# Two heads side by side: 64-wide products of a recurrence and an attention regrouped

## The chip, the cores and the metric

One core of one Trainium2 chip runs the whole program in one launch. The metric is device time in microseconds (us), the median of three runs. The engines are TensorE (PE in the rows; PEld is its weight load), VectorE (DVE), ScalarE (ACT), GpSimd (POOL) and SyncE (SP), which issues the loads of the weights.

## The reference, cut to what matters

Three transformer blocks follow each other on one sequence of 256 tokens with 2048 features, all in float32. Blocks 2 and 3 are not touched. Block 1 normalises x, multiplies by `w_in`, and runs two branches of 16 heads with 64 features each, a gated linear recurrence and an attention:

```python
# recurrence, a 64 x 64 state per head, token by token
kk = (k * k_k).reshape(B, S, H, N)
kk = kk / jnp.maximum(jnp.sqrt(jnp.sum(kk * kk, axis=-1, keepdims=True)), 1e-12)
def step(state, inp):
    rt, wt, kt, vt, kkt, at = inp
    sa = jnp.einsum('bhvk,bhk->bhv', state, -kkt)
    state = (state * wt[:, :, None, :] + sa[..., None] * (kkt * at)[:, :, None, :]
             + vt[..., :, None] * kt[..., None, :])
    return state, jnp.einsum('bhvk,bhk->bhv', state, rt)
# y is then normalised per token and head (mean and variance over its 64 features)

# attention of a chunk of 64 tokens to itself and the chunks before it
s = jnp.einsum('bqhd,bkhd->bhqk', qc, kc) + bias          # invalid keys: -1e30
p = jax.nn.softmax(s, axis=-1)
o = jnp.einsum('bhqk,bkhd->bqhd', p, vc)
```

## The kernel before, in words

`run` is the weight stream. Each weight tile of 128 × 1024 is loaded by SP, split into a high part `whi` (ScalarE, L209) and a low part `wlo` (VectorE, L210), and multiplied with an activation that stands as high and low parts too: L249 (512 columns) and L250 (256 columns) alternate on TensorE for each block of 128 × 128 weights. The four accumulators `pm` have four of the eight PSUM banks.

Everything else is a background task, a Python generator. After each unit of the stream (four pairs L249/L250 in the common form) `step` lets every task issue its next stage; `yield n` leaves out steps. So the work of a task stands between the stream's products in the order in which it was issued, and each engine works in that order; `run` and `step` write it out, no scheduler moves it. Tiles come from pools and wait for the release of the buffer that they get: `PS` (four PSUM banks for all background tasks), `X` (five tiles; the scores `sc`, `E`, `BT` and `UV` are among them), `T` (12), `Q` (30 large tiles).

`attention` starts one head every three steps: scores `psc` (two products on 64 rows of the array, the row half by the head's parity, L337, L338), bias and maximum on VectorE, exponentials on ScalarE, scaling on POOL, three transposes `ptr`, a copy, and two products with v into `ppv` (L365, L366), each head into its 64 columns. Block 1 calls it twice with eight heads (`att`); blocks 2 and 3 call it with heads of 128.

`rwkv(hf)` runs the recurrence of eight heads, so twice. Four tiles i hold two heads each (par 0 on partitions 0 to 63, par 1 on 64 to 127). First come the decay and rate from `w2` (`pw`, `pa`, L741, L742) and the inverse norm `rn` of kk, which four products per tile spread over the features (`pkk`, L786); the operands `AR` and `BK`; a triangular inverse `Z`. Then four chunks c of 64 tokens. `gram(c)` makes the masked products P (`pgr`, L912), `BT` (four full transposes `pbt`, L918) and v token-major (`pvt`, L925, products with pieces of the identity). The chunk then does `pW` (from the state S, L943, and from P, L945), `pU` (with Z, L954), the next state's `pS` (L964) and the output `pY` (from P, L978, and from the state, L981). `group_norm` normalises pY and turns it feature-major (`pyt`, L1030).

Of the kernel before, what the change touches and what calls it, by code (L numbers as in the profile page):

```python
# [10 lines left out]
ALU = mybir.AluOpType  # L11
# [6 lines left out]
# columns of the packed per-feature vectors (each vector of n features takes n / 128 columns)  # L18
# [27 lines left out]
class FM:  # L46
    """A feature-major tensor [128 * n, 256] as tiles of four rows of blocks."""
# [8 lines left out]
class HL:  # L56
    """An activation (hi | lo), two blocks of 128 features to a tile."""
# [8 lines left out]
class Builder:  # L66
# [102 lines left out]
    def get(self, key, f):  # L169
        """Block f of the (hi | lo) activation st[key], once it is on its way."""  # L170
# [3 lines left out]
    def start(self, gen):  # L174
        """First stage of what happens to a product; the further ones follow, one a step."""
# [4 lines left out]
    def run(self, panels):  # L180
# [39 lines left out]
        for i, (p, g) in enumerate(groups):  # L220
# [12 lines left out]
            # where, among the units of this group, the next group is split  # L233
# [34 lines left out]
    def sum_halves(self, p):  # L268
        """The product of a weight tile: its two halves in PSUM, added."""
# [8 lines left out]
    def split_act(self, dst, src):  # L278
        """dst (hi | lo) of src, both parts exact."""
# [4 lines left out]
    def scaled_split(self, dst, src, g):  # L284
        """dst (hi | lo) of src * g, g one number per partition."""
# [10 lines left out]
    def sum_sq(self, accs):  # L296
        """Sums over partitions and tiles ([128, 256] each), token-major, in PSUM [128, 2]."""
# [15 lines left out]
    def bcast_psum(self, rt):  # L313
        """A token-major [128, 2], over all partitions: [128, 256]."""
# [12 lines left out]
    def attention(self, heads, q, k, v, bias, dim, out):  # L327
        """Softmax attention of query tiles (tokens 0-127 on keys 0-127, 128-255 on 0-255).
        q, k: feature-major [dim, 256]; v(h, t): token-major [128, dim]; bias(h, s, p) is a task that
        writes s [128, 384] = scores + bias; out(i, psum [128, 256])."""  # L330
        nc = self.nc
        pvs, done = {}, []

        def head(h):
            p = self.PS("psc")
            qa, ka = q(h), k(h)
            nc.tensor.matmul(p[:, 0:128], qa[:, 0:128], ka[:, 0:128], start=True, stop=True)  # L337
            nc.tensor.matmul(p[:, 128:384], qa[:, 128:256], ka, start=True, stop=True)  # L338
            s = self.X("sc", [128, 384])
            yield from bias(h, s, p)  # L340
            mx = self.SM([128, 2], "mx")
            nc.vector.tensor_reduce(out=mx[:, 0:1], in_=s[:, 0:128], axis=AX.X, op=ALU.max, negate=True)
            nc.vector.tensor_reduce(out=mx[:, 1:2], in_=s[:, 128:384], axis=AX.X, op=ALU.max, negate=True)
            yield 2
            sm = self.SM([128, 2], "sm")
            nc.scalar.activation(s[:, 0:128], s[:, 0:128], AF.Exp, bias=mx[:, 0:1], accum_out=sm[:, 0:1])
            nc.scalar.activation(s[:, 128:384], s[:, 128:384], AF.Exp, bias=mx[:, 1:2], accum_out=sm[:, 1:2])
            yield 2
            rs = self.SM([128, 2], "rs")
            nc.vector.reciprocal(rs, sm)  # L350
            nc.gpsimd.tensor_scalar(s[:, 0:128], s[:, 0:128], rs[:, 0:1], None, op0=ALU.mult)
            nc.gpsimd.tensor_scalar(s[:, 128:384], s[:, 128:384], rs[:, 1:2], None, op0=ALU.mult)
            yield 3
            p = self.PS("ptr")
            nc.tensor.transpose(p[:, 0:128], s[:, 0:128], self.ident)
            nc.tensor.transpose(p[:, 128:256], s[:, 128:256], self.ident)
            nc.tensor.transpose(p[:, 256:384], s[:, 256:384], self.ident)
            yield 2
            nc.scalar.copy(s, p[:, 0:384])
            yield 2  # L360
            if dim == 128 or h % 2 == 0:
                pvs[h * dim // 128] = self.PS("ppv")
            pv = pvs[h * dim // 128]
            o = pv[(h * dim) % 128:(h * dim) % 128 + dim, 0:256]
            nc.tensor.matmul(o, v(h, 0), s[:, 0:256], start=True, stop=False, skip_group_check=True)  # L365
            nc.tensor.matmul(o[:, 128:256], v(h, 1), s[:, 256:384], start=False, stop=True,  # L366
                             skip_group_check=True)
            if dim == 128 or h % 2:
                yield 2
                out(h * dim // 128, pv[:, 0:256])  # L370
            done.append(h)

        for h in heads:
            self.bg(head(h))
            yield 3
# [4 lines left out]
    def block1_constants(self):  # L380
# [19 lines left out]
        # 1 - x of mu_r, mu_k, mu_v and of k_a  # L400
# [5 lines left out]
    def input_norm(self, x, gname, hl, key):  # L406
        """hl (hi | lo) of x * g, four blocks at a time, then st[key]: sums of squares."""
# [17 lines left out]
    def load_x(self, name, between=False):  # L425
        """x, feature-major; the later tiles between the first tiles of the weights, or at once."""
# [10 lines left out]
    def block1(self):  # L437
# [36 lines left out]
        # attention, eight heads at a time: q, k feature-major, v token-major  # L474
# [44 lines left out]
        # LoRA: (h + (shift(h) - h) mu) w = h ((1 - mu) w) + shift(h) (mu w)  # L519
# [23 lines left out]
        def mixed(key, n, hf):  # L543
            """y + (shift(y) - y) mu of the product y"""
# [25 lines left out]
        # gated attention branch  # L570
# [70 lines left out]
        # merged branches  # L641
# [59 lines left out]
    def residual(self, hl, gname, key):  # L701
        """x += rms(o) post_norm_g; hl of x * g for what follows; st[key] of 1 / rms(x)."""
# [24 lines left out]
    def rwkv(self, hf):  # L727
        """The recurrence of eight heads, in chunks of 64 tokens."""
# [4 lines left out]
        # decay and in-context rate  # L733
# [16 lines left out]
        # 1 / max(|k k_k|, 1e-12) per head  # L750
# [16 lines left out]
        rn = self.SM([128, 2, 8], "rn")  # L767
        nc.gpsimd.tensor_tensor(rn.rearrange("p t h -> p (t h)"), mn, self.mhalf[:, 0:16], op=ALU.pow)
# [7 lines left out]
        def operands(i):  # L776
# [46 lines left out]
        # (I - L)^-1 per head and chunk: diagonal blocks of 32 by substitution, one block per partition  # L823
# [58 lines left out]
        # the block below the diagonal: X21^T = X11^T L21^T X22^T  # L882
# [19 lines left out]
        # the recurrence over chunks  # L902
        Pt, BT, UV = {}, {}, {}

        def gram(c):
            P_ = Pt[c] = self.Q("P", [128, 2, 4, 128])
            m = self.mask1[:, None, :].to_broadcast([128, 4, 128])
            for par in range(2):
                o = slice(par * 64, par * 64 + 64)
                p = self.PS("pgr")  # L910
                for i in range(4):
                    nc.tensor.matmul(p[:, i * 128:(i + 1) * 128], bk(i, c)[o, :], ar(i, c)[o, :], start=True, stop=True)  # L912
                yield
                nc.vector.tensor_tensor(P_[:, par], p.rearrange("p (i t) -> p i t", i=4), m, op=ALU.mult)
# [6 lines left out]
            U_ = UV[c] = self.X("UV", [128, 4, 2, 64])  # L921
            p = self.PS("pvt")
            for i in range(4):
# [797 lines left out]
```

## Time and profile before

| | us |
|---|---|
| median of three runs | 3351.51 (3348.92 to 3356.8) |
| profiled execution: span from first to last instruction | 3342.3 |
| TensorE busy in it | 3288.9 (98%) |
| VectorE, ScalarE, POOL busy | 2066.9 (62%), 1716.4 (51%), 556.2 (17%) |
| mean granted TensorE clock, as a share of 2.4 GHz | 0.994 |

The profile gives no other time of the profiled execution than its span. Its rows show a float32 product of the code as two records on TensorE (two passes over the columns) and a transpose as one. A shape such as 64*128 64x128 says 64 rows and 128 columns of the array, and the operand's partitions and columns. Lengths overlap, since a product begins while the one before runs out; starts are the better guide.

### The profile page before, as it was taken

How to read it: one execution, taken by the hardware profiler on the slowest of the kernel's cores; microseconds unless marked ns; L12 is line 12 of the kernel's file. 1: busy time of each engine (PE TensorE's matmuls, PEld its weight loads, DVE VectorE, ACT ScalarE, POOL GpSimd, SP SyncE). 2: the span in 40 equal slices, each digit the busy share in tenths (PEclk: the TensorE clock that was granted, in tenths of full speed). 3: DMA queues.
4: the chain of work that ended last, by engine and by line, in shares of the span. 5: the costliest groups of instructions: out<-in, count | busy, mean ns of one | idle time of the engine just before them, and what ended most of it. 6: DMA issues, size and time to landing. Idle time of an engine off the chain costs nothing.

```text
span 3342.3 us, 50547 instructions
## 1 busy us (share of the span) xinstructions
PE 3288.9 (98%) x19438; PEld 2826.5 (85%) x19438; DVE 2066.9 (62%) x3034; ACT 1716.4 (51%) x2868; POOL 556.2 (17%) x568
## 2 busy tenths in 40 slices
PE   8999999999989999999999999999999999999998
PEld 7787888888878888888888888888888888888887
DVE  5577657646476546576555555658757755565556
ACT  5454544435444574455545545456455654545454
POOL 2132131204130322233100000004224300000001
PEclk9999999999989999999999999999999999999999
DMA  6555535535545555656565556565555556655564
GB/s 205 167 160 162 158 95 170 164 120 188 190 131 172 184 156 183 196 184 187 184 200 189 185 188 196 189 189 184 183 178 166 184 185 188 195 189 189 188 191 145
DMA packets 175585, 589.91 MB, mean 177 GB/s; under 512 B 28784, under 2 KB 31984, under 8 KB 175344
## 3 DMA queue, kind: packets, MB, share of 16 engines
q1 hardware_dynamic: 174624, 585.47, 55.8%
q8 instruction: 152, 2.49, 0.3%
q10 hardware_dynamic: 720, 1.22, 0.1%
q14 instruction: 89, 0.73, 0.1%
HBM read 582.95 MB, written 3.67 MB: 176 GB/s over the span
## 4 chain that ended last, share of the span: by engine, by line
PE 76%; DVE 4%; issue 3%; ACT 2%; POOL 1%; DVEq 0%; POOLq 0%; ACTq 0%
PE pm L249 45%; PE pm L250 23%; DVE wlo L210 2%; PE pm L255 1%; PE pm L257 1%; PE pm L256 1%; ACT whi L209 1%; DVE ev L275 0%; PE ppv L365 0%; POOL ev L661 0%; PE pgr L912 0%; PE psc L338 0%; PE pY L978 0%; PE ppl L1591 0%; DVE mr L1344 0%
## 5 line engine op out<-in xcount | busy, mean ns | idle before, releaser
L210 DVE TENSOR_TENSOR wlo<-wf,whi 128x1024 fp32r<-128x1024 f32 x1086 | 1349.4, 1266 | 1128.6 <-ACT whi L209 1109.2
L249 PE MATMUL pm<-h,whi 128*128 128x512 f32 x3872 | 1376.0, 398 | 12.9 <-ACT whi L209 8.7
L209 ACT CAST whi<-wf 128x1024 fp32r<-128x1024 f32 x1086 | 1107.2, 1050 | 479.8 <-PE pm L249 391.3
L250 PE MATMUL pm<-h,wlo 128*128 128x256 f32 x3872 | 1087.9, 281 | 6.7 <-DVE wlo L210 6.6
L249 PEld LDWEIGHTS pm<-h,whi 128*128 128x128 f32 x3872 | 727.0, 188 | 188.9 <-ACT whi L209 9.0
L250 PEld LDWEIGHTS pm<-h,wlo 128*128 128x128 f32 x3872 | 733.3, 189 | 12.1 <-DVE wlo L210 11.5
L249 PE MATMUL pm<-hid,whi 128*128 128x512 f32 x2048 | 710.8, 391 | 0.0
L250 PE MATMUL pm<-hid,wlo 128*128 128x256 f32 x2048 | 573.3, 280 | 0.0
L272 ACT COPY ev<-pm 128x256 f32<-128x256 f32 x491 | 181.2, 369 | 695.5 <-PE pm L250 679.8
L249 PEld LDWEIGHTS pm<-hid,whi 128*128 128x128 f32 x2048 | 383.1, 187 | 84.6
L249 PE MATMUL pm<-hb,whi 128*128 128x512 f32 x1168 | 421.0, 403 | 11.4 <-DVE hb L717 8.6
L250 PEld LDWEIGHTS pm<-hid,wlo 128*128 128x128 f32 x2048 | 387.0, 189 | 0.0
L1072 POOL TENSOR_TENSOR acc<-acc,sqa 128x256 f32<-128x256 f32 x104 | 120.2, 1162 | 1496.0 <-ACT sqa L1067 1472.5
L250 PE MATMUL pm<-hb,wlo 128*128 128x256 f32 x1168 | 330.1, 283 | 1.3 <-DVE wlo L210 1.1
L249 PEld LDWEIGHTS pm<-hb,whi 128*128 128x128 f32 x1168 | 221.4, 190 | 68.3 <-issue 8.7
L250 PEld LDWEIGHTS pm<-hb,wlo 128*128 128x128 f32 x1168 | 223.4, 191 | 4.2 <-DVE wlo L210 3.1
L275 DVE TENSOR_TENSOR ev<-pm,ev 128x256 f32<-128x256 f32 x491 | 198.9, 416 | 27.0 <-ACT ev L272 26.8
L249 PE MATMUL pm<-mg,whi 128*128 128x512 f32 x512 | 179.6, 395 | 0.0
L250 PE MATMUL pm<-mg,wlo 128*128 128x256 f32 x512 | 143.8, 281 | 1.0 <-DVE wlo L210 1.0
L249 PEld LDWEIGHTS pm<-mg,whi 128*128 128x128 f32 x512 | 96.0, 187 | 22.6
L250 PEld LDWEIGHTS pm<-mg,wlo 128*128 128x128 f32 x512 | 96.7, 189 | 1.7 <-DVE wlo L210 1.6
L255 PE MATMUL pm<-whi,hb 128*128 128x512 f32 x160 | 66.0, 412 | 0.0
(353 smaller groups left out, 3099.9 us busy)
## 6 DMA issues: line engine op xcount, KB each, us to landing
wf<-w_in SPq DMA_DIRECT2D x312, 512.0 KB, 4.0
wf<-w_ff SPq DMA_DIRECT2D x256, 512.0 KB, 4.4
wf<-w_sgu SPq DMA_DIRECT2D x128, 512.0 KB, 3.9
wf<-w_up SPq DMA_DIRECT2D x128, 512.0 KB, 4.4
wf<-w_down SPq DMA_DIRECT2D x128, 512.0 KB, 4.3
wf<-w_out SPq DMA_DIRECT2D x96, 512.0 KB, 4.3
wf<-w_branch_attn SPq DMA_DIRECT2D x16, 512.0 KB, 3.6
wf<-w_branch_rwkv SPq DMA_DIRECT2D x16, 512.0 KB, 4.1
```

Of the source, the lines that this page charges most:

```text
L209: self.nc.scalar.copy(hi, t)
L210: self.nc.vector.tensor_tensor(lo, t, hi.bitcast(F32), op=ALU.subtract)
L249: mm(out, hi[:, c], a, start=st, stop=False, skip_group_check=True)
L250: mm(out[:, 256:512], lo[:, c], a[:, 0:256], start=False, stop=en, skip_group_check=True)
L255: mm(o, ah, hi, start=st, stop=False, skip_group_check=True)
L256: mm(o, ah, lo, start=False, stop=False, skip_group_check=True)
L257: mm(o, al, hi, start=False, stop=en, skip_group_check=True)
L272: nc.scalar.copy(a, p[:, 256:512])
L275: nc.vector.tensor_tensor(b, p[:, 0:256], a, op=ALU.add)
L1072: nc.gpsimd.tensor_tensor(accs[0], accs[0], s, op=ALU.add)
```

## The change

Block 1's small products are put together in other groups; what is computed is the same.

- `attention`: a unit is now 128/dim heads, two in block 1. The scores of both stand in one burst, alternating between the row halves and in two banks, and likewise the `ppv` of both. Each stage of the other engines does both heads; a unit starts every six steps.
- `pkk`: POOL writes rn out as `rx` (128 × 1024), and two products on the whole array take the place of four on 64 columns.
- `gram`: both parities of `pgr` in one burst of eight products that alternate between the row halves; both masks follow. v is turned by full transposes, two chunks at once (in chunks 0 and 2), and four copies put the quarters in place, two on ScalarE, two on VectorE.
- Chunk: the state's part of pY is issued with pW, the P part with pS; pU lies in the other half of pW's bank and pS in that of pY's, so pY holds its bank from pW until the group norm has read it.
- `group_norm`: two full transposes for eight products, and four copies (two on ScalarE, two on VectorE) for one.

The norm, in `rwkv` and `operands`:

```diff
+        rx = self.Q("rx", [128, 2, 512])
+        nc.gpsimd.tensor_copy(rx.rearrange("p t (h n) -> p (t h) n", n=64), rn[:, :, None].to_broadcast([128, 16, 64]))
         yield 5
...
             for t in range(2):
-                for u in range(2):
-                    nc.tensor.matmul(pk[u * 64:u * 64 + 64, t * 128:(t + 1) * 128],
-                                     rn[:, t, 2 * i + u:2 * i + u + 1].to_broadcast([128, 64]), self.ident,
-                                     start=True, stop=True)
+                nc.tensor.matmul(pk[:, t * 128:(t + 1) * 128],
+                                 rx[:, t, i * 128:(i + 1) * 128], self.ident,
+                                 start=True, stop=True)
```

The unit of `attention` (the stages between are those of one head, each done for both):

```diff
+        def unit(hs):
+            ps = [self.PS("psc") for _ in hs]
+            for a in (0, 128):
+                for h, p in zip(hs, ps):
+                    qa, ka = q(h), k(h)
+                    nc.tensor.matmul(p[:, a:2 * a + 128], qa[:, a:a + 128], ka[:, 0:a + 128], start=True, stop=True)
+            ss = [self.X("sc", [128, 384]) for _ in hs]
...
+            for s in ss:
+                p = self.PS("ptr")
+                for c in range(0, 384, 128):
+                    nc.tensor.transpose(p[:, c:c + 128], s[:, c:c + 128], self.ident)
                 yield 2
+                nc.scalar.copy(s, p[:, 0:384])
+            yield 2
+            pv = self.PS("ppv")
+            os = [pv[(h * dim) % 128:(h * dim) % 128 + dim, 0:256] for h in hs]
+            for h, s, o in zip(hs, ss, os):
+                nc.tensor.matmul(o, v(h, 0), s[:, 0:256], start=True, stop=False, skip_group_check=True)
+            for h, s, o in zip(hs, ss, os):
+                nc.tensor.matmul(o[:, 128:256], v(h, 1), s[:, 256:384], start=False, stop=True, skip_group_check=True)
```

`gram`:

```diff
+            ps = [self.PS("pgr") for _ in range(2)]
+            for i in range(4):
+                for par in range(2):
+                    o = slice(par * 64, par * 64 + 64)
+                    nc.tensor.matmul(ps[par][:, i * 128:(i + 1) * 128], bk(i, c)[o, :], ar(i, c)[o, :],
+                                     start=True, stop=True)
+            yield
             for par in range(2):
-                o = slice(par * 64, par * 64 + 64)
-                p = self.PS("pgr")
-                for i in range(4):
-                    nc.tensor.matmul(p[:, i * 128:(i + 1) * 128], bk(i, c)[o, :], ar(i, c)[o, :], start=True, stop=True)
-                yield
-                nc.vector.tensor_tensor(P_[:, par], p.rearrange("p (i t) -> p i t", i=4), m, op=ALU.mult)
+                nc.vector.tensor_tensor(P_[:, par], ps[par].rearrange("p (i t) -> p i t", i=4), m, op=ALU.mult)
...
-                for o in (0, 64):
-                    nc.tensor.matmul(p[o:o + 64, i * 64:(i + 1) * 64], v[i][o:o + 64, c * 64:(c + 1) * 64],
-                                     self.ident[o:o + 64, o:o + 64], start=True, stop=True)
+            if c % 2 == 0:
...
+                    nc.tensor.transpose(p[:, i * 128:(i + 1) * 128], v[i][:, c * 64:(c + 2) * 64], self.ident)
```

The chunk:

```diff
+            pw, py = self.PS("pW"), self.PS("pY")
...
+            if c:
+                for i in range(4):
+                    for par, f, w in halves:
+                        nc.tensor.matmul(py[f, i * 64:(i + 1) * 64], ar(i, c)[f, 64:128], Sp[f, i, :], start=i == 0,
+                                         stop=False, skip_group_check=True)
...
-            pu = self.PS("pU")
+            pu = pw[:, 256:512]
...
+            pS = py[:, 256:512]
+            for i in range(4 if c < 3 else 0):
+                for par, f, w in halves:
+                    nc.tensor.matmul(pS[f, i * 64:(i + 1) * 64], B_[:, i, f], U_[:, i, par, :], start=not c and i == 0,
+                                     stop=True, skip_group_check=True)
+            for i in range(4):
+                for par, f, w in halves:
+                    nc.tensor.matmul(py[f, i * 64:(i + 1) * 64], P_[:, par, i, 64:128], U_[:, i, par, :], start=False,
+                                     stop=True, skip_group_check=True)
+            yield
```

`group_norm`:

```diff
-        for i in range(4):
-            for o in (0, 64):
-                nc.tensor.matmul(p[o:o + 64, i * 64:(i + 1) * 64], yc[o:o + 64, i, :],
-                                 self.ident[o:o + 64, o:o + 64], start=True, stop=True)
+        for j in range(2):
+            nc.tensor.transpose(p[:, j * 128:(j + 1) * 128], yc[:, 2 * j:2 * j + 2, :].rearrange("p i t -> p (i t)"), self.ident)
```

In the rows below, L numbers of the changed kernel are its own, the number behind a name tells buffers apart, and "..." stands for the stream's products.

TensorE, chunk 1 of the first half, before:

```order
L943 MATMUL pW<-S,AR 64x64
L945 MATMUL pW<-UV,P 64x64
...
L954 MATMUL pU<-ws,Z 64x64 x8
...
L964 MATMUL pS<-UV,BT 64x64 x8
...
L978 MATMUL pY<-UV,P 64x64
L981 MATMUL pY<-S,AR 64x64
...
```

The same chunk now:

```order
L966 MATMUL pW<-S,AR 64x64 x2
L969 MATMUL pW<-UV,P 64x64 x2
...
L974 MATMUL pY<-S,AR 64x64 x8
...
L983 MATMUL pW<-ws,Z 64x64 x8
...
L993 MATMUL pY<-UV,BT 64x64 x8
L997 MATMUL pY<-UV,P 64x64 x8
```

The state's part of pY has moved from behind pS to behind pW, and pU (now in pW) and pS (now in pY) write banks that are already taken.

TensorE, `gram(0)` of the first half, before:

```order
L912 MATMUL pgr_3718<-AR_1994,BK_1996 128x128 x2
L912 MATMUL pgr_3718<-AR_1995,BK_1997 128x128 x2
...
L912 MATMUL pgr_3740<-AR_1994,BK_1996 128x128 x2
...
L918 MATMUL pbt_3758<-ident_79,BK_1996 128x128 x2
...
L925 MATMUL pvt_3777<-ident_79,pv0_1483 64x64 x8
```

And now:

```order
L925 MATMUL pgr_3728<-AR_2008,BK_2010 128x128
L925 MATMUL pgr_3729<-AR_2008,BK_2010 128x128
...
L933 MATMUL pbt_3752<-ident_79,BK_2010 128x128 x2
L933 MATMUL pbt_3752<-ident_79,BK_2011 128x128 x2
...
L942 MATMUL pvt_3772<-ident_79,pv0_1483 128x128 x4
```

The two parities' banks alternate in one burst, and one burst between the stream's units is gone.

TensorE with its waits, the second half's decay and rate (pw, pa) within chunk 1 of the first half, before:

```order
L943 MATMUL pW_4051<-S_3907,AR_1994 64x64 [waits DVE_49]
L945 MATMUL pW_4051<-UV_4013,P_3935 64x64 [waits Activation_49]
...
L741 MATMUL pw_4091<-lora_871,w2_899 128x256 [waits PE_49]
L742 MATMUL pa_4092<-lora_871,w2_899 128x256 [waits Activation_49]
...
L954 MATMUL pU_4120<-ws_4084,Z_3450 64x64 [waits Activation_49]
```

And now:

```order
L751 MATMUL pw_4039<-lora_875,w2_908 128x256
L752 MATMUL pa_4040<-lora_875,w2_908 128x256 [waits Activation_49]
...
L983 MATMUL pW_3971<-ws_4012,Z_3460 64x64 [waits Activation_49]
L983 MATMUL pW_3971<-ws_4012,Z_3460 64x64 x7
...
L751 MATMUL pw_4089<-lora_875,w2_908 128x256 [waits DVE_49]
L752 MATMUL pa_4090<-lora_875,w2_908 128x256 [waits Activation_49]
```

With pW and pY both held, the second pair's `pa` takes the bank of the first pair's `pw`, and its wait on ScalarE is for the second sigmoid that reads that bank.

## Rows read from the trace of the kernel before

**Rows 1.** The page, part 1: engine, busy us, share of the span, instructions.

```profile
PE 3288.9 (98%) x19438; PEld 2826.5 (85%) x19438; DVE 2066.9 (62%) x3034; ACT 1716.4 (51%) x2868; POOL 556.2 (17%) x568
```

**Rows 2.** The page, part 4: shares of the span by engine and line.

```profile
PE pm L249 45%; PE pm L250 23%; DVE wlo L210 2%; PE pm L255 1%; PE pm L257 1%; PE pm L256 1%; ACT whi L209 1%; DVE ev L275 0%; PE ppv L365 0%; POOL ev L661 0%; PE pgr L912 0%; PE psc L338 0%; PE pY L978 0%; PE ppl L1591 0%; DVE mr L1344 0%
```

**Rows 3.** Timeline of TensorE from 378 us: start, length, line, operation, shapes, count.

```profile
378.04 0.28 PE L250 MATMUL pm<-h,wlo 128*128 128x256 f32 x1
378.24 1.16 PE L912 MATMUL pgr<-AR,BK 64*128 64x128 f32 x8
...
379.66 0.28 PE L250 MATMUL pm<-h,wlo 128*128 128x256 f32 x1
...
380.01 0.28 PE L250 MATMUL pm<-h,wlo 128*128 128x256 f32 x1
...
383.39 0.28 PE L250 MATMUL pm<-h,wlo 128*128 128x256 f32 x1
383.51 0.60 PE L918 MATMUL pbt<-ident,BK 128*128 128x128 f32 x4
...
384.18 0.28 PE L250 MATMUL pm<-h,wlo 128*128 128x256 f32 x1
...
385.45 0.68 PE L925 MATMUL pvt<-ident,pv 64*64 64x64 f32 x16
```

**Rows 4.** Stretches, L250 alone: us, busy PE (count), PEld (count), clock, DMA, GB/s.

```profile
378.00:510.00 132.00, 62.54 (x220) 42.30 (x220) 0.97 0.36 110
625.00:750.00 125.00, 64.90 (x231) 44.09 (x231) 0.99 0.40 123
```

**Rows 5.** Timeline of TensorE, 213 us, pkk.

```profile
213.38 0.66 PE L786 MATMUL pkk<-ident,rn 128*64 128x128 f32 x8
```

**Rows 6.** Timeline of TensorE, 672 us, pY of a later chunk: first two and last row.

```profile
672.00 0.33 PE L978 MATMUL pY<-UV,P 128*64 128x64 f32 x2
672.25 0.33 PE L981 MATMUL pY<-S,AR 64*64 64x64 f32 x2
...
675.85 0.32 PE L981 MATMUL pY<-S,AR 64*64 64x64 f32 x2
```

**Rows 7.** Timeline of TensorE, 412 us, pW of a later chunk: first and last row.

```profile
412.68 0.34 PE L943 MATMUL pW<-S,AR 64*64 64x64 f32 x4
...
413.54 0.33 PE L945 MATMUL pW<-UV,P 64*64 64x64 f32 x4
```

**Rows 8.** Timeline of TensorE, 397 us, pS.

```profile
397.74 0.69 PE L964 MATMUL pS<-UV,BT 128*64 128x64 f32 x16
```

**Rows 9.** Timeline of TensorE, 181 us, products on alternating row halves.

```profile
181.44 0.38 PE L741 MATMUL pw<-lora,w 64*128 64x256 f32 x1
181.45 0.38 PE L742 MATMUL pa<-lora,w 64*128 64x256 f32 x1
181.66 0.38 PE L741 MATMUL pw<-lora,w 64*128 64x256 f32 x1
```

**Rows 10.** Timeline of TensorE, scores and value products of one head.

```profile
87.31 0.49 PE L337 MATMUL psc<-k,q 64*128 64x128 f32 x2
87.64 0.59 PE L338 MATMUL psc<-k,q 64*128 64x256 f32 x2
...
114.90 0.65 PE L365 MATMUL ppv<-sc,vt 128*64 128x256 f32 x2
115.38 0.38 PE L366 MATMUL ppv<-sc,vt 128*64 128x128 f32 x2
```

**Rows 11.** Stretch, all engines; the granted clock is third from last.

```profile
431.20:434.60 3.40, 3.40 (x12) 2.46 (x12) 0.00 (x0) 0.00 (x0) 0.00 (x0) 0.50 0.46 157
```

**Rows 12.** Timeline of ScalarE at 414 us.

```profile
414.30 1.28 ACT L746 ACT_TABLE_LOAD   x1
415.59 0.48 ACT L746 ACTIVATE sg<-pw,vecs 128x256 f32<-128x256 f32 x1
```

**Rows 13.** VectorE by line, 75 to 760 us: count, busy us, mean ns, idle before.

```profile
L914 DVE TENSOR_TENSOR P<-pgr,mask 128x512 f32<-128x512 f32 x16 | 11.0, 688 | 22.0 <-PE pgr L912 21.9
```

More of the change, by code (lines that the diff above doesn't have):

```diff
@@ L1 @@
 import math
+from itertools import zip_longest
 from contextlib import ExitStack
@@ L373, in attention @@
-        for h in heads:
-            self.bg(head(h))
-            yield 3
+        done = []
+        def unit(hs):
[5 more added lines that the diff above has]
+            ss = [self.X("sc", [128, 384]) for _ in hs]
+            for b in zip_longest(*(bias(h, s, p) for h, s, p in zip(hs, ss, ps))):
+                yield max(n or 1 for n in b)
+            mxs = []
+            for s in ss:
+                mx = self.SM([128, 2], "mx")
+                mxs.append(mx)
+                nc.vector.tensor_reduce(out=mx[:, 0:1], in_=s[:, 0:128], axis=AX.X, op=ALU.max, negate=True)
+                nc.vector.tensor_reduce(out=mx[:, 1:2], in_=s[:, 128:384], axis=AX.X, op=ALU.max, negate=True)
+            yield 2
+            sms = []
+            for s, mx in zip(ss, mxs):
+                sm = self.SM([128, 2], "sm")
+                sms.append(sm)
+                nc.scalar.activation(s[:, 0:128], s[:, 0:128], AF.Exp, bias=mx[:, 0:1], accum_out=sm[:, 0:1])
+                nc.scalar.activation(s[:, 128:384], s[:, 128:384], AF.Exp, bias=mx[:, 1:2], accum_out=sm[:, 1:2])
+            yield 2
+            for s, sm in zip(ss, sms):
+                rs = self.SM([128, 2], "rs")
+                nc.vector.reciprocal(rs, sm)
+                nc.gpsimd.tensor_scalar(s[:, 0:128], s[:, 0:128], rs[:, 0:1], None, op0=ALU.mult)
+                nc.gpsimd.tensor_scalar(s[:, 128:384], s[:, 128:384], rs[:, 1:2], None, op0=ALU.mult)
+            yield 3
+            for s in ss:
+                p = self.PS("ptr")
[3 more added lines that the diff above has]
+                nc.scalar.copy(s, p[:, 0:384])
+            yield 2
+            pv = self.PS("ppv")
[4 more added lines that the diff above has]
+                nc.tensor.matmul(o[:, 128:256], v(h, 1), s[:, 256:384], start=False, stop=True, skip_group_check=True)
+            yield 2
+            out(hs[0] * dim // 128, pv[:, 0:256])
+            done.extend(hs)
@@ L376, in attention @@
+        n = 128 // dim
+        for i in range(0, len(heads), n):
+            self.bg(unit(heads[i:i + n]))
+            yield 3 * n
         while len(done) < len(heads):
@@ L973, in rwkv @@
                     nc.vector.tensor_tensor(Sn, i4(pS), dc, op=ALU.mult)
-            py = self.PS("pY")
-            for i in range(4):
-                for par, f, w in halves:
-                    o = py[f, i * 64:(i + 1) * 64]
-                    nc.tensor.matmul(o, P_[:, par, i, 64:128], U_[:, i, par, :], start=True, stop=not c,
-                                     skip_group_check=True)
-                    if c:
-                        nc.tensor.matmul(o, ar(i, c)[f, 64:128], Sp[f, i, :], start=False, stop=True,
-                                         skip_group_check=True)
-            yield
             self.bg(self.group_norm(i4(py), v.t[0][:, :, c * 64:(c + 1) * 64], (hf, c)))
@@ L1027, in group_norm @@
         p = self.PS("pyt")
-        for i in range(4):
-            for o in (0, 64):
-                nc.tensor.matmul(p[o:o + 64, i * 64:(i + 1) * 64], yc[o:o + 64, i, :],
-                                 self.ident[o:o + 64, o:o + 64], start=True, stop=True)
+        for j in range(2):
+            nc.tensor.transpose(p[:, j * 128:(j + 1) * 128], yc[:, 2 * j:2 * j + 2, :].rearrange("p i t -> p (i t)"), self.ident)
         yield
-        nc.scalar.copy(out, p[:, 0:256].rearrange("p (i t) -> p i t", i=4))
+        o4 = out.rearrange("p (j e) t -> p j e t", e=2)
+        p4 = p[:, 0:256].rearrange("p (j h t) -> p j h t", j=2, h=2)
+        for e in range(2):
+            for par in range(2):
+                dst, src = o4[par * 64:par * 64 + 64, :, e, :], p4[e * 64:e * 64 + 64, :, par, :]
+                if par:
+                    nc.vector.tensor_copy(dst, src)
+                else:
+                    nc.scalar.copy(dst, src)
         self.st[("gn",) + key] = True
```

71 lines of the change are left out of this document (21 added, 50 removed).

## The prediction

> **What bounds the kernel now.** I read the page's busy shares first: TensorE is busy 98% of a span of 3342.3 us [rows 1]. The chain of waits then says with what: 45% and 23% of the span are lines L249 and L250, the weight stream [rows 2], so no other engine sets the end for long. The timeline shows how the stream runs when nothing comes between: from one L250 to the next 0.35 us (379.66 to 380.01) [rows 3]. Last I counted the stream in two stretches of block 1. From 625 to 750 us, which hold the second half's recurrence, 231 pairs ran; at 0.353 us they need 81.5 us, so 43.5 of 125 us went to small matmuls set between them; from 378 to 510 us 220 pairs leave 54 of 132 us [rows 4]. Every microsecond that those small bursts lose or gain is one of the end, as long as ScalarE and VectorE keep the stream fed.
>
> **What a burst costs.** The distance between the L250 before and the L250 after it, less 0.35. For the first Gram burst (L912, four products, eight passes) that is 379.66 − 378.04 − 0.35 = 1.27 us, 0.11 more than the 1.16 us its row lasts [rows 3]. Bursts of 64-wide tiles all have that tail (the array runs empty on the way in and out), so I add 0.11 to a row's length; where a burst has several rows, from the start of the first to the end of the last. Transposes on the full array are cheap: four of 128 columns cost 384.18 − 383.39 − 0.35 = 0.44, one pass each, no tail [rows 3].
>
> **The change, part by part** (us; before minus after, over both halves).
>
> Transposes of v (pvt): now 8 products a chunk in eight bursts of 0.68 + 0.11 = 0.79 [rows 3], 6.3. Then four bursts of four full transposes at 0.44, 1.8. Gain 4.5. The normalised y (pyt) has bursts of the same form, eight of them, 6.3; then two full transposes, half of 0.44, eight times, 1.8. Gain 4.5. Both are priced by a row of the same operation.
>
> pkk: eight bursts of 0.66 + 0.11 = 0.77 [rows 5], 6.2. Then two full products, four passes of 128 columns, as the four transposes have: 0.44, 3.5. Gain 2.7; no gain if such a pass took twice as long, 3 at best. The copy that spreads rn over 64 columns (rx) stands on POOL, with five steps of stream behind it before its reader, so I cost it at nothing; if it came late, pkk would wait.
>
> Recurrence. For chunks 1 to 3 the output burst pY alternates products of 128 and of 64 rows; each change of shape takes a quarter of a microsecond (672.00, 672.25), 16 rows until 675.85 + 0.32: 4.17 + 0.11 = 4.28 [rows 6]. Six of them are 25.7. pW of these chunks lasts 412.68 to 413.87, 1.19 + 0.11 = 1.30 [rows 7], six are 7.8. pS is 0.69 + 0.11 = 0.80 [rows 8], six are 4.8, and the two pY of chunk 0, of the same form, 1.6. Together 39.9. Afterwards no burst changes shape inside: eight AR products join pW, eight P products join pS. Eight products more in one shape cost pW's 1.30 less the 0.80 of a burst of eight, 0.50. So 6 × 1.80, 6 × 1.30 and, for the last chunks, 2 × 0.80: 20.2. Gain 19.7; 16.1 if each added group cost a whole burst, 21 if 0.4.
>
> Here a rule speaks against it. In the 64-wide bursts of before, two row halves write one bank of PSUM at different partitions: pvt, 16 passes of 64 columns in 0.68 [rows 3]. By a transpose's 0.11 for 128 columns [rows 3] they would need 0.88 one after another, so they overlap. The Trainium skill (TensorEngine Tiling (Array Packing), Restrictions and Gotchas, Gotcha 1) says that different row tiles can't access one PSUM bank at the same time; pvt's row disagrees. By the rule the six added AR groups, which write pY's one bank from both row halves, would run singly, 0.88 instead of 0.50, and the sum would be 2.3 us smaller.
>
> Two heads side by side. Of the Gram's two parities the products now alternate between the row halves, and so do the scores (psc) of two heads; the ppv of two heads alternates between column halves. That two halves run together is shown: pw and pa start 0.01 us apart, each 0.38 long, and the next two 0.22 later [rows 9].
> - Gram: 16 × 1.27 = 20.3. After it eight bursts of 16 passes: at best 8 pairs at half of 0.22, 1.0 with the tail; at worst 2 × 1.16 + 0.11 = 2.43. The nearest row is pkk's, eight 128-column passes that alternate between two halves in 0.66 [rows 5]; twice that less one run-out, about 1.3. Gain 9.9 (0.9 to 12).
> - Scores: 87.31 to 88.23 is 0.92 + 0.11 = 1.03 [rows 10], times 16 is 16.5. After: eight bursts of 1.03 at best, 1.95 if one head follows the other. I take 1.10, as pw and pa bear out the overlap. Gain 7.7 (0.9 to 8.2).
> - ppv: 114.90 to 115.76 is 0.86 + 0.11 = 0.97 [rows 10], 15.5. After, 0.97 to 1.83, I take 1.05. Gain 7.1 (0.9 to 7.8).
>
> Sum: 4.5 + 4.5 + 2.7 + 19.7 + 9.9 + 7.7 + 7.1 = 56.1. pbt, pU, and the attention's three transposes stay. My prices agree with the count: for 625 to 750 us they add up to about 44, with the clock below.
>
> Clock. From 431.2 us the granted clock is 0.50, that is 1.2 GHz, for 3.4 us [rows 11]; the means of the two stretches, 0.97 and 0.99 [rows 4], hold two more such dips, at 444.9 and 704.3. Two of the three begin while a pY burst with its sixteen changes of shape is running. Half speed for 3.4 us costs 1.7. With those bursts gone I count two dips, 3.4 us, as gained (0 to 5.1).
>
> New waits. (a) The four banks of the background pool. pU now lies in pW's bank and pY's is taken from pW until the group norm has read it. In chunk 1 of the first half the second pw/pa pair finds its bank only when two sigmoids of the first pair have read it: ScalarE has behind pU's copy a table load of 1.28 and three sigmoids of up to 0.48 [rows 12], so it is done some 3 us after pU, and TensorE is there after four pairs, 1.4. It waits about 1.5, with the stream behind it. Before, this pair found a bank free. (b) The masks of both parities (0.69 each) [rows 13] are now issued together, a step after pgr and just ahead of pbt; pW or pvt waits for them. Between lie two steps of four pairs and pbt, 3.3 us, for 1.4 of masks and whatever VectorE has before them, such as a weight's low part. (c) The halves of v leave their bank by copies on ScalarE and VectorE in turn, issued just ahead of pW, which needs two of them. (d) Five tiles hold scores; two heads a unit and up to three units in flight need six. So a bias addition on VectorE waits for the ppv of the unit two before, and the next low part of a weight stands behind it; the stream waits for that. For (b) to (d), at twenty-odd places with slack mostly over a microsecond, I take 3.5, between 0 and 12. All waits: 5.
>
> Result: 56.1 + 3.4 − 5 = 54.5. The profiled span of 3342.3 would be 3287.8. The page gives no time for that execution beyond its span; the median of the runs, 3351.5, is 9.2 longer, which I leave as it is: 3351.5 − 54.5 = 3297.0.
>
> **Rivals.**
> *No overlap.* The halves are issued alternately but run singly, for instance because a pass must wait for its own weights. pw and pa speak against it for row halves; pkk only in part for column halves, and no row shows 128-column passes on row halves. Then Gram, scores and ppv give 2.7 instead of 24.7, in all 32.5: 3319.
> *The other engines are late.* For: a chunk now takes nine or ten steps instead of twelve, and VectorE is in order. Against: TensorE waits for almost nothing today [rows 1]. If each of 28 such places (eight pairs of masks, eight units of two heads, four bursts of v, eight of y) costs a microsecond more, 28 us go: 3325. The Trainium skill (the same page, Performance Considerations, PSUM Bottleneck) states that tiling speeds up TensorE but not the emptying of PSUM, which may then be the bound; no row here shows it yet.
> *Slower: the banks.* One mechanism: pY keeps a bank from pW to the group norm, so pbt or pvt of the next chunk meets a bank that an instruction behind VectorE's queue must free. If VectorE is a whole weight group behind, four low parts, TensorE stands at each of the eight chunks until it has caught up. The change turns slower from 59.5 us in all, 7.4 a chunk; at 8 a chunk it is 3351.5 − 59.5 + 64 = 3356. Against it: from pgr to the waiting product lie 3.3 us, and VectorE has gaps.
> *No change.* Only if the weight stream were held elsewhere in block 1; rows 4 speak against it, since what isn't stream there is bursts.
>
> **How the numbers follow.** Forecast 0.66, no overlap 0.12, late engines 0.14, no change 0.03, slower 0.05. A measurement of this kernel tells some 0.2%, 6.7 us, from no change. Faster: 0.66 + 0.12 + 0.14 = 0.92; same 0.03; slower 0.05. The forecast's own range is 3286 (all halves at the best pace, third dip gone, waits 1) to 3310 (waits 12 and half of the overlap lost on ppv and Gram). To hold eight in ten it reaches to no overlap and part of the late engines: 3286 to 3326.
>
> **What will show it.** In the profile after: pY rows without a change of shape inside, and none of their bursts over 2.2 us; a Gram burst of sixteen passes near 1.2 long (2.3 would be no overlap); psc and ppv of two heads each about 1 us; fully busy stretches of TensorE, with its waits on VectorE and ScalarE in block 1 below 6 us; one wait of about 1.5 at the second pa (L752); no clock of 0.50 behind the pY bursts. The stream's count shows the sum: 231 pairs in about 104 instead of 125 us. The forecast is wrong if the bursts shrink as said and the waits grow by as much, or if the clock falls elsewhere.

## The result and the profile after

The changed kernel takes 3309.92 us (median of 4 runs, 3309.41 to 3314.03) against 3350.22 for the kernel before on the same chip: ratio 0.9874 [0.9857, 0.9892], 40.3 us faster. The forecast was 3297, 54.5 faster. The profiled execution of after took 3309.79 us with a span of 3307.9; between the profiled spans lie 34.4 us (the execution of before that was profiled, span 3342.3, is shorter than all four of its timed runs, which exceed their spans by about 1.9). Lines of after are 1 higher in the stream (L250 and L251 for L249 and L250); other lines are given as they come.

The page, part 1 (the line that answers to [rows 1]), and the two stretches that answer to [rows 4], low parts alone (L251: us, busy PE (count), PEld (count), clock, DMA, GB/s):

```profile
PE 3238.6 (98%) x19182; PEld 2797.5 (85%) x19182; DVE 2076.2 (63%) x3058; ACT 1710.5 (52%) x2868; POOL 560.0 (17%) x570
```
```profile
371.70:493.00 121.30, 63.03 (x220) 42.58 (x220) 0.97 0.40 120
610.24:716.30 106.06, 65.00 (x231) 43.58 (x231) 1.00 0.47 144
```

The same 220 pairs of the first half took 132.0 us before and take 121.3; the 231 of the second half 125.0 and 106.1, where 104 were forecast. So the second half nearly gave what was expected (18.9 of 21 us), the first little more than half as much (10.7).

The bursts themselves, from TensorE's timeline (start, length, line, operation, shapes, count), which answer to [rows 3, 6, 7, 10]:

```profile
85.92 0.93 PE L341 MATMUL psc<-k,q 64*128 64x128 f32 x8
...
115.66 0.65 PE L375 MATMUL ppv<-sc,vt 128*64 128x256 f32 x4
116.14 0.39 PE L377 MATMUL ppv<-sc,vt 128*64 128x128 f32 x4
...
371.94 1.16 PE L925 MATMUL pgr<-AR,BK 64*128 64x128 f32 x16
...
388.58 0.69 PE L993 MATMUL pY<-UV,BT 128*64 128x64 f32 x16
389.09 0.64 PE L997 MATMUL pY<-UV,P 128*64 128x64 f32 x16
...
445.26 0.28 PE L251 MATMUL pm<-yah,wlo 128*128 128x256 f32 x1
...
446.33 0.22 PE L974 MATMUL pY<-S,AR 64*64 64x64 f32 x1
...
446.34 0.22 PE L974 MATMUL pY<-S,AR 64*64 64x64 f32 x1
...
447.18 0.28 PE L251 MATMUL pm<-yah,wlo 128*128 128x256 f32 x1
```

Two heads of scores take 0.93 where one took 0.92, two heads of ppv 0.87, both parities of Gram products 1.16 like one parity before. No burst of pY changes shape inside; pW with its eight added AR products costs 447.18 − 445.26 − 0.35 = 1.57.

What was given back stands in the view of waits (TensorE, 242 to 720 us: who waited, for whom, us in total, times, longest). After:

```profile
PE pm L251 <- DVE wlo L211: 14.3, 13, 3.1
PE pW L969 <- ACT UV L951: 1.5, 1, 1.5
PE pm L250 <- DVE ev L276: 1.3, 3, 0.8
PE pW L969 <- DVE UV L949: 1.2, 2, 0.9
PE pm L250 <- ACT whi L210: 1.1, 1, 1.1
PE pw L751 <- DVE UV L987: 1.0, 1, 1.0
PE pvt L942 <- DVE P L929: 0.7, 1, 0.7
```

Before, the same view:

```profile
PE pm L250 <- DVE wlo L210: 4.4, 7, 0.8
PE pm L249 <- DVE ev L275: 3.4, 4, 1.5
PE pbo L809 <- DVE ku L803: 1.2, 1, 1.2
PE pm L249 <- ACT whi L209: 0.4, 1, 0.4
```

21.1 against 9.4 us, and the longest waits are new. Behind each of these waits that is longer than 1.7 us (423.42 and 424.07 together are one) TensorE runs at half clock (1.2 GHz); the timeline's waits, and stretches in which it does (the granted clock is third from last; it falls 0.3 us before the wait at 268.56 ends, and 0.4 to 1.9 us behind the others):

```profile
268.56 0.58 PE L251 MATMUL pm<-h,wlo 128*128 128x256 f32 x1 [3.08 <-DVE wlo L211]
345.89 0.39 PE L251 MATMUL pm<-h,wlo 128*128 128x256 f32 x1 [2.00 <-DVE wlo L211]
423.42 0.33 PE L969 MATMUL pW<-UV,P 64*64 64x64 f32 x2 [1.45 <-ACT UV L951]
424.07 0.27 PE L969 MATMUL pW<-UV,P 64*64 64x64 f32 x1 [0.33 <-DVE UV L949]
476.10 0.39 PE L251 MATMUL pm<-h,wlo 128*128 128x256 f32 x1 [1.95 <-DVE wlo L211]
583.89 0.38 PE L251 MATMUL pm<-h,wlo 128*128 128x256 f32 x1 [1.75 <-DVE wlo L211]
```
```profile
268.60:275.40 6.80, 6.33 (x20) 5.07 (x21) 5.91 (x17) 4.06 (x10) 3.71 (x4) 0.52 0.60 187
347.10:350.50 3.40, 3.13 (x10) 2.72 (x11) 3.40 (x8) 0.00 (x0) 0.00 (x0) 0.54 0.85 245
425.60:429.00 3.40, 3.40 (x12) 2.87 (x13) 2.69 (x3) 1.88 (x4) 1.00 (x1) 0.54 0.27 48
476.80:480.20 3.40, 3.40 (x12) 2.78 (x12) 3.37 (x10) 1.93 (x4) 3.05 (x5) 0.54 0.50 157
586.10:589.50 3.40, 3.40 (x13) 2.87 (x13) 1.68 (x2) 0.00 (x0) 0.00 (x0) 0.55 0.70 202
```

Before, block 1 had three stretches of 3.4 us at 0.50 [rows 11]; after it has 20.4 us. At half speed 20.4 us lose 10.2, where 10.2 us lost 5.1.

The longest wait, at 268.56, has a history on VectorE, which works in order:

```profile
250.82 1.23 DVE L211 TENSOR_TENSOR wlo<-wf,whi 128x1024 fp32r<-128x1024 f32 x1 [4.73 <-ACT whi L210]
251.96 0.68 DVE L848 TENSOR_TENSOR LT<-pLT,mask 128x512 f32<-128x512 f32 x1
...
265.18 0.29 DVE L503 TENSOR_TENSOR sc<-psc,b 128x128 f32<-128x128 f32 x1 [9.28 <-POOL b L500]
```

The second mask of LT, an operand of the triangular inverse, stands behind a low part that waits 4.73 us; the DMAs that copy LT (to `d`, then to LD) wait for the mask, the bias tile's DMA stands behind them on SP (issued at 258.04), and the first bias addition waits 9.28 us for it with the next low part queued behind. In the kernel before the mask stood ahead of that low part (255.00 and 259.59). What moved it is one added `yield` ahead of rx, which the lines of the change ahead of the prediction do not show; it puts everything after it a step later in the stream.

### The profile page after: what moved, and what is told of

Read it like the earlier page. It is cut to its first block, busy times and chain, and to the rows that moved or that the text cites. A ratio compares the mean times of both kernels' runs of the same rounds, so it can differ in the third digit from the quotient of the medians.

```text
span 3307.9 us, 50068 instructions
## 1 busy us (share of the span) xinstructions
PE 3238.6 (98%) x19182; PEld 2797.5 (85%) x19182; DVE 2076.2 (63%) x3058; ACT 1710.5 (52%) x2868; POOL 560.0 (17%) x570
## 4 chain that ended last, share of the span: by engine, by line
PE 86%; DVE 6%; issue 3%; ACT 3%; POOL 1%; DMA 0%; DVEq 0%; POOLq 0%; ACTq 0%
PE pm L250 51%; PE pm L251 26%; DVE wlo L211 3%; PE pm L256 2%; PE pm L258 2%; PE pm L257 2%; ACT whi L210 2%; PE psc L341 1%; DVE ev L276 0%; PE ppv L375 0%; PE ptr L368 0%; POOL ev L671 0%; PE pst L302 0%; PE ppl L1622 0%; DMA b<-bias 0%
## 5 line engine op out<-in xcount | busy, mean ns | idle before, releaser
L250 PE MATMUL pm<-h,whi 128*128 128x512 f32 x3872 | 1377.0, 398 | 11.1 <-ACT whi L210 7.8
L251 PE MATMUL pm<-h,wlo 128*128 128x256 f32 x3872 | 1091.4, 282 | 16.1 <-DVE wlo L211 15.6
L250 PEld LDWEIGHTS pm<-h,whi 128*128 128x128 f32 x3872 | 729.6, 188 | 181.5 <-ACT whi L210 8.2
L251 PEld LDWEIGHTS pm<-h,wlo 128*128 128x128 f32 x3872 | 735.4, 190 | 24.9 <-DVE wlo L211 24.2
L250 PE MATMUL pm<-hid,whi 128*128 128x512 f32 x2048 | 711.2, 391 | 0.0
L251 PE MATMUL pm<-hid,wlo 128*128 128x256 f32 x2048 | 573.5, 280 | 0.0
L250 PEld LDWEIGHTS pm<-hid,whi 128*128 128x128 f32 x2048 | 383.1, 187 | 84.8
L250 PE MATMUL pm<-hb,whi 128*128 128x512 f32 x1168 | 419.3, 401 | 12.1 <-DVE hb L727 9.2
L251 PEld LDWEIGHTS pm<-hid,wlo 128*128 128x128 f32 x2048 | 387.1, 189 | 0.0
L251 PE MATMUL pm<-hb,wlo 128*128 128x256 f32 x1168 | 329.6, 282 | 1.4 <-DVE wlo L211 1.1
L250 PEld LDWEIGHTS pm<-hb,whi 128*128 128x128 f32 x1168 | 220.9, 189 | 68.2 <-issue 9.5
L251 PEld LDWEIGHTS pm<-hb,wlo 128*128 128x128 f32 x1168 | 223.0, 191 | 4.1 <-DVE wlo L211 2.9
L250 PE MATMUL pm<-mg,whi 128*128 128x512 f32 x512 | 178.0, 391 | 0.0
L251 PE MATMUL pm<-mg,wlo 128*128 128x256 f32 x512 | 143.7, 281 | 0.9 <-DVE wlo L211 0.9
L250 PEld LDWEIGHTS pm<-mg,whi 128*128 128x128 f32 x512 | 95.8, 187 | 21.2 <-DVE ev L276 0.2
L251 PEld LDWEIGHTS pm<-mg,wlo 128*128 128x128 f32 x512 | 96.8, 189 | 1.9 <-DVE wlo L211 1.9
```

What stands on the lines that cost most here:

```text
L250: mm(out, hi[:, c], a, start=st, stop=False, skip_group_check=True)
L251: mm(out[:, 256:512], lo[:, c], a[:, 0:256], start=False, stop=en, skip_group_check=True)
```

## The experiments

The theory: the bursts became as short as forecast, and the missing gain was given back by VectorE and ScalarE being asked a step too early or in a worse order, and a second time by the clock that falls behind such a wait. The main rival: the two-head units themselves make VectorE late.

**e1: the added step taken out.**

```diff
         rx = self.Q("rx", [128, 2, 512])
         nc.gpsimd.tensor_copy(rx.rearrange(...), rn[:, :, None].to_broadcast([128, 16, 64]))
-        yield 5
+        yield 4
```

> The changed kernel with one step fewer between the spread of rn (rx) and the operands (yield 4 for yield 5), so that everything behind it stands at the same step of the stream as in the kernel before. Theory: the added step put the second LT mask behind a weight's low part that waits 4.7 us for a slot; the DMA of d1, LD and the bias tile then start late, VectorE waits 9.3 us for the bias tile, the stream waits 3.1 us for a low part and runs 6.8 us at 1.2 GHz. With the step gone the wait for L500 is under 5 us, the 3.1 and the 3.4 of the clock vanish: 5 to 7 us faster than the changed kernel, about 3304. Rival (two heads a unit load VectorE too much at the start of attention 1, whatever the step): within 2 us of the changed kernel, about 3310.

3302.85 us (before 3352.31 on the chip of e1 to e4), ratio 0.9855 [0.983, 0.988], 7.1 below the changed kernel's median, 9.2 if each is taken against its own before. The intervals of the two ratios overlap, so the trace has to decide. The mask is 5 us earlier, and the wait for the bias tile is 3.81 (VectorE):

```profile
246.90 0.69 DVE L848 TENSOR_TENSOR LT<-pLT,mask 128x512 f32<-128x512 f32 x1
251.50 1.23 DVE L211 TENSOR_TENSOR wlo<-wf,whi 128x1024 fp32r<-128x1024 f32 x1 [3.91 <-ACT whi L210]
...
260.38 0.29 DVE L503 TENSOR_TENSOR sc<-psc,b 128x128 f32<-128x128 f32 x1 [3.81 <-POOL b L500]
```

From the first psc of the second attention to its last ppv 63.4 us became 56.6: 6.8 gone, the wait of 3.1 and the half clock of 6.8 us with it. As the theory said. The span of this execution (3308.5) is no shorter than the changed kernel's, for it was the slowest of e1's four runs: counted from the stream's first product, it is 6.3 us ahead of after behind the last changed burst (at the product that stands at 775.1 us in before), and loses some 7 in block 2, which the edit leaves alone (from 1400 to 1600 us 1140 matmul records for 1155, at clock 1.00 in both; why stays open).

**e2: the attention alone** (the kernel before with the new `unit(hs)` in place of `head(h)`).

> The kernel before with nothing but the attention's units of two heads. Theory (attention is worth its 14.8 us and was held up in the changed kernel by the shifted bias DMA alone): attention 0 gives 6, attention 1 gives 6 to 7, 12 to 14 us faster than the kernel before, about 3338. Rival (the units themselves make VectorE late at attention 1): attention 1 gives nothing, 5 to 6 us faster, about 3345.

3334.45 us, ratio 0.9951 [0.9934, 0.9969], 17.9 faster than before; the interval holds the theory's 12 to 14 and shuts out the rival's 5 to 6. From pLT to pT, the stretch with the second attention, it takes 109.1 us where the kernel before took 115.9 and the changed one 118.0. Its waits of TensorE, 242 to 720 us, are below those of before:

```profile
PE pm L250 <- DVE ev L276: 3.8, 4, 1.8
PE pm L251 <- DVE wlo L211: 2.7, 5, 0.7
```

So the two-head units add no wait of TensorE. But the clock falls for 23.9 us in this stretch of time, more than in any other run, and only one of the five falls (337.7) has a wait over 0.7 us beside it. The other four (446.9, 481.1, 662.0, 692.7; 20.5 us) begin inside a pY burst with its changes of shape, or within 0.5 us behind one; e2 still has these bursts. The first of the four (clock third from last):

```profile
446.90:453.70 6.80, 6.80 (x31) 5.21 (x31) 0.01 (x1) 1.09 (x2) 0.00 (x0) 0.50 0.25 77
```

**e3: everything but the attention** (the changed kernel with the old `head(h)`).

> The changed kernel with the attention of the kernel before: recurrence, Gram products, transposes and pkk changed alone. Its bursts by the measured lengths save about 43 us. Theory: the added step still makes the bias tile late (4 to 6 us lost in attention 1) and the recurrence waits for its copies and masks (6 to 8): about 30 us faster than the kernel before, 3317 to 3323. Rival (the waits come from the units of two heads): nearly the whole 43, about 3308.

3323.36 us, ratio 0.9914 [0.9893, 0.9935], 29.0 faster than before, at the slow end of the theory's numbers and 15 from the rival's. It has the changed kernel's waits (14.2 us for low parts in 14 places, pW 2.6, pw 1.0), and pLT to pT takes 121.8; the second mask stands behind a low part that waits 4.74, and VectorE waits 9.15 for the bias tile: the added step costs with the old attention too. Its waits of 2.55, 2.54 and 1.96 us for low parts (358.80, 488.35, 597.30) leave the clock at 1.00, and it has only 6.8 us at half clock.

**e4: Gram products one parity after the other.**

```diff
-            for i in range(4):
-                for par in range(2):
+            for par in range(2):
+                for i in range(4):
                     o = slice(par * 64, par * 64 + 64)
                     nc.tensor.matmul(ps[par][:, i * 128:(i + 1) * 128], bk(i, c)[o, :], ar(i, c)[o, :],
```

> The changed kernel with the Gram products issued one parity after the other (all of row half 0, then all of row half 1) instead of alternating; the same products, banks and masks. Theory (the two row halves overlap only when issued alternately): a burst goes from 1.28 to about 2.3 us, eight times 1.0 to 1.1, 8 to 9 us slower than the changed kernel, about 3318. Rival (the saving came from fewer bursts, not from overlap): under 2 us slower.

3313.82 us, ratio 0.989 [0.9869, 0.9911], 3.9 above the changed kernel, 1.8 if each is taken against its own before; the intervals overlap. The row grew from 1.16 to 1.71:

```profile
373.43 1.71 PE L925 MATMUL pgr<-AR,BK 64*128 64x128 f32 x16
```

Eight times 0.55 is 4.4, and at the product named under e1 this trace is 4.2 behind after. Neither number held: two bursts before cost 2 × 1.27 = 2.54, one burst in series 1.71 + 0.11 = 1.82, the alternating one about 1.3. Of the gain per chunk 0.7 comes from one interruption fewer and 0.55 from the overlap. I had put the price of running singly too high, in the prediction (2.43) as here, by counting the start-up of a burst twice.

**e5: e1 with more steps ahead of pW.**

```diff
                         else:
                             nc.scalar.copy(dst, src)
+                yield 2
+            else:
+                yield
```

> e1 with two more steps between the copies of v (UV) and pW in the even chunks, one more step between the copy of pbt and pW in the odd ones. Theory: the stream's gain was given back by products that come a step too early for VectorE and ScalarE, and once more by the clock that falls behind each such wait. The waits of pW for UV (1.9, 0.6 and 0.5 us in e1) and for P (1.0) go, and with them the 6.8 us at 1.2 GHz at 413.5: 5 to 8 us faster than e1, about 3296. Rival (VectorE and ScalarE simply have too much to do in this stretch): the waits move to the weights' low parts, within 2 us of e1.

3290.51 us (before 3349.47 on the chip of e5 to e8), ratio 0.9826 [0.9813, 0.984], 12.3 below e1, or 9.5 if each is taken against its own before (59.0 and 49.5): more than expected. Its waits, 242 to 720 us:

```profile
PE pm L250 <- DVE ev L276: 3.9, 4, 1.8
PE pm L251 <- DVE wlo L211: 3.3, 7, 0.7
PE pm L250 <- DVE ua L619: 2.6, 1, 2.6
PE pw L751 <- ACT sg L756: 1.6, 1, 1.6
```

pW waits no more, the half clock at 413.6 is gone, and the low parts wait less (3.3 for 9.0), not more: the rival falls. No work was taken from VectorE or ScalarE; a chunk only takes a step or two longer. What appears is the wait that the prediction called (a), 1.6 for a sigmoid, at pw, where 1.5 was forecast at pa.

**e6: e5 with three steps between the two pw/pa pairs of the second half.**

```diff
                 nc.scalar.activation(aa[i + u], pa[:, o], AF.Sigmoid, bias=self.vec("a0", f0 + i + u))
+            if hf and not i:
+                yield 3
```

> e5 with three more steps between the first pair of pw/pa of the second half and the second pair. Theory: the second pair and the Gram products behind it no longer stand before sigmoids and copies that are still to come (0.2 at pa, 0.6 at pgr in e1, 1.9 in the changed kernel's burst of pw): 1 to 3 us faster than e5. Rival: the bank is free by then anyway once e5's steps are in, no difference within 1 us.

3289.75 us, ratio 0.9824 [0.981, 0.9837]: 0.8 below e5, which the intervals do not tell apart. The wait of 1.6 is gone from the trace, but the later operands then stand elsewhere and meet a wait of 1.9 for a low part. Inconclusive in time.

**e7: e6 with the second attention's first bias tile loaded at the start of the panel of v.**

```diff
+                           pre=(lambda hf=hf: load_bias(2 * hf)) if hf else None, post=(lambda hf=hf: self.bg(att(hf)))))
```

> e6 with the bias tile of the second attention's first group loaded when the panel of v starts, some 25 us earlier. Theory: with the step gone (e1) the wait of VectorE for this tile no longer reaches the stream, so it shortens VectorE's wait from about 4 us to nothing and the time by less than 1 us. Rival (the late tile still costs the stream): 2 to 4 us faster than e6.

3286.83 us, ratio 0.9816 [0.9803, 0.983]: 2.9 below e6, again within the intervals, so theory and rival are not told apart. It is the fastest kernel here, 62.6 below the one before, where the change alone gave 40.3. Its second half:

```profile
595.97:699.50 103.53, 64.64 (x231) 43.63 (x231) 1.00 0.46 143
```
TensorE waits 10.3 us from 242 to 720 us, about as before the change (5.7 of it for low parts, at most 1.9 at once), and has one stretch of 3.4 us at half clock in block 1: the 231 pairs take the 104 us that the prediction named.

**e8: waits of growing length in an otherwise full stretch.**

```diff
+            if p.w is self.aps["w_ff1_2"]:
+                nff += 1
+                if nff % 8 == 4:
+                    t = self.T("dm")
+                    for _ in range(6 + 3 * (nff // 8)):
+                        nc_.vector.tensor_tensor(t, self.vecs[:, 0:256], self.vecs[:, 0:256], op=ALU.add)
```

> e1 with bursts of 6, 9, 12 ... 27 additional additions on VectorE (128x256, some 0.33 us each, results unused), each ahead of one low part, eight weight groups apart, in the first feed-forward product of block 2, where TensorE otherwise runs the stream alone at full clock. Theory: the low parts come late by growing amounts; a wait of TensorE under 1 us costs only itself, from about 1.4 us on the granted clock falls to 0.50 right behind it for 3.4 us and costs 1.7 us more, and longer waits have 6.8 us at 0.50. Rival (the falls of the clock in block 1 come from the small tiles or their changes of shape, not from the waits): no stretch at 0.50 in the feed-forward.

One run, 3326.71 us. The last four of the eight delays reached TensorE (timeline), with these stretches beside them:

```profile
1940.33 0.47 PE L257 MATMUL pm<-h,whi 128*128 128x512 f32 x1 [1.12 <-DVE ev L283]
1987.81 0.47 PE L257 MATMUL pm<-h,whi 128*128 128x512 f32 x1 [2.71 <-DVE ev L283]
2129.25 0.76 PE L257 MATMUL pm<-h,whi 128*128 128x512 f32 x1 [3.87 <-DVE ev L283]
2181.32 0.77 PE L257 MATMUL pm<-h,whi 128*128 128x512 f32 x1 [5.25 <-DVE ev L283]
```
```profile
1940.30:1944.00 3.70, 3.67 (x20) 3.12 (x21) 2.76 (x5) 3.63 (x8) 0.00 (x0) 1.00 0.72 204
1989.00:1992.40 3.40, 3.40 (x12) 2.92 (x13) 2.47 (x5) 3.33 (x8) 0.00 (x0) 0.51 0.74 248
2129.00:2132.40 3.40, 3.15 (x10) 2.73 (x11) 2.47 (x6) 3.19 (x8) 0.00 (x0) 0.52 0.67 194
2180.20:2187.00 6.80, 5.68 (x18) 4.91 (x19) 5.87 (x10) 5.63 (x13) 0.00 (x0) 0.51 0.66 167
```

1.12 us cost no clock, 2.71 and 3.87 us 3.4 us of half speed, 5.25 us 6.8. There are no small tiles in this stretch, so a wait alone can be enough. It need not be: up to block 2 e8 is e1, with the same two waits at pW (1.88 and 0.64 in e1, 1.87 and 0.64 here). In e1 6.8 us at 0.50 followed, here none:

```profile
412.52 0.32 PE L976 MATMUL pW<-UV,P 64*64 64x64 f32 x2 [1.87 <-ACT UV L958]
```
```profile
412.50:419.30 6.80, 6.14 (x72) 5.17 (x74) 5.04 (x10) 4.12 (x8) 1.01 (x1) 1.00 0.40 97
```

The delays came through the sums that empty the stream's banks (L283), not through the low parts.

## Why the prediction was right in the bursts and wrong in what surrounds them

The sum against the trace, from psc of the first attention to the last pyt. "Bursts" are the distances between the stream's rows around each burst, less the undisturbed pitch, added up: 139.7 us before, 91.0 after, 83.5 in e7.

| term | predicted | between the profiled spans |
|---|---|---|
| bursts | +56.1 | +56.2 (139.7 − 83.5; inside them e7 has only the wait of 1.2 at pbo that before has too) |
| clock | +3.4 | −5.1 (10.2 us at half speed, then 20.4) |
| waits | −5 | −16.7 (what is left of 34.4; 11.7 of it in the view of waits) |
| all | 54.5 | 34.4 |

- **Bursts: right.** Scores, Gram and recurrence come at or below their prices: 1.04 for 1.10, 1.30 for 1.30, 1.57 for 1.80 (pW), 1.28 for 1.30 (pY). "No overlap" falls by these rows; e4 shows that it would have cost some 4 us at Gram, not the 9 I gave it. The rule of the Trainium skill (TensorEngine Tiling (Array Packing), Restrictions and Gotchas, Gotcha 1) that different row tiles can't access one PSUM bank at the same time would have made the pW burst longer than forecast; it is shorter, and products of both row halves into pY's bank start 0.01 us apart (446.33, 446.34).
- **Clock: wrong in sign.** The falls at pY's bursts went, as forecast, and e2 bears out that they go with those bursts (20.5 us at half clock beside them, where the profiled execution of before had 6.8). The step that failed is "With those bursts gone I count two dips, 3.4 us, as gained": it has no term for what a new wait does. From 242 to 720 us in all ten traces, and in e8's ladder, a stretch at 0.50 begins in, or within 2 us behind, 18 of 22 waits of TensorE of 1.74 us or more, and five of 23 between 1.1 and 1.65, each with another wait of 0.3 to 0.8 close by. The four that kept the clock are e3's three (up to 2.55) and e8's 1.87. So a wait of that length mostly cost 1.7 us more than itself, and whether it did changed from one execution to the next with the same code: e1 against e8, or pbo, which waits 2.30 in after (231.71) and keeps the clock, and 2.32 in e4 and loses it.
- **Waits: (a) to (d) at 5 were too small, and one was missing.** (a), the shortage of banks, came near its price: 1.6 in e5, and 1.0 in after, there for VectorE's copy out of pU and not for a sigmoid. (b) and (c) are there: 0.7 at pvt, 2.7 at pW. (d), the tiles and bias additions of two heads, is nothing for TensorE (e2; VectorE waits once for a ppv, 1.0). The largest was not on the list: "The copy that spreads rn over 64 columns (rx) stands on POOL ... so I cost it at nothing". The copy is free, but its `yield` moves all that follows by one step, and this put one mask behind a waiting low part: 6.8 us (e1). The steps that the shorter chunks leave out cost another 9.5 (e5, each kernel against its own before), where (b) to (d) had 3.5.
- **The rivals.** The time lies at the slow edge of the forecast's own range (3310), but not for that edge's reasons: no overlap was lost, and waits and clock together took 21.8 where that edge takes 12 for waits, counts the clock as a gain and puts the rest on lost overlap (its parts, 54.5 − 7 − 7.6, make 3312, not 3310). That the range held is luck in part. The time is 12.9 above the forecast and 15 below "the other engines are late" (3325), and that rival's mechanism is what happened, at fewer places and with the clock on top. The Trainium skill's rule named there (the same page, Performance Considerations, PSUM Bottleneck), that a faster TensorE may leave the emptying of PSUM as the bound, is borne out in part: pW's 2.7 us wait for copies out of pvt's bank. But e5 removes them without taking away a copy, so the order is the bound, not the amount. The banks never held a chunk for 8 us, so "slower" falls.

Open: of the 16.7 us of waits the view shows 11.7, and pbo ahead of it 1.1 (2.30 against 1.17). Of the 3.9 that remain, 2.0 lie in after's own bursts (91.0, or 84.3 without the waits of 6.7 inside them, against e7's 82.3); the rest I could not place. And a wait is not the only thing that stands before a fall: e6 has 3.4 us at half clock at 426.1 with no wait beside it over 0.3 us, behind a pss burst of 1.95 us (423.35, products of 2 columns); of the three of before two begin inside pY bursts and one (444.9) just behind pss (442.43). No run has one of these bursts alone, so that they cause the falls is not shown.

## What to carry to other kernels

When bursts on the bound engine get shorter, every helper engine is asked sooner: price the waits anew at each place, and give steps back where the chain has room (e5: three steps a pair of chunks, 9.5 us). Count a `yield` as an edit of its own, since on an in-order queue one place later can mean behind an instruction that waits. And add to a long wait of TensorE (here from about 1.7 us) the time that the half clock mostly costs behind it.

## What the runs showed of the hardware that was not expected

A TensorE that is 98% busy can still lose its clock to one wait: 2.71 us, once, gave 3.4 us at 1.2 GHz, 5.25 us gave 6.8 (e8). The same waits at the same place did so in one execution (e1) and not in another (e8), so the profiles of two executions differ by some microseconds for this alone. Sixteen 64-row passes of 128 columns (eight float32 products) take 1.16 us when the row halves alternate and 1.71 in series (e4), so the overlap is worth a third of the row, not half.
